# Weight sums of a Strassen feed-forward by accumulating DMAs instead of vector instructions

## The chip, the cores and the metric

The kernel runs on one core of a Trainium2 chip. The metric is the device time of one execution in microseconds; the median of three runs counts. The engines are TensorE (PE, with PEld for its weight loads), VectorE (DVE), ScalarE (ACT), GpSimd (POOL) and SyncE (SP), which issues most DMAs. Each engine works through its own queue in order; semaphores tie the queues together.

## The reference

A decoder trunk of two pre-norm layers on 512 tokens of width 1024, with 16 learned tokens put in front (L = 528). Layer 0 mixes tokens by causal pooling, layer 1 by stick-breaking attention. Each layer ends with a feed-forward part of 2816 hidden features, which is what the change touches. All is float32.

```python
def swiglu(h, w_gate, w_up, w_down):
    return (jax.nn.silu(h @ w_gate) * (h @ w_up)) @ w_down
...
    for i in range(DEPTH):
...
        h = h + mix
        h = h + swiglu(rmsnorm(h, norm_ffn[i]), ffn_w_gate[i], ffn_w_up[i], ffn_w_down[i])
    h = rmsnorm(h, final_norm)
    return h[:, N_META:]
```

## The kernel before

Activations lie feature-major: `hT` is eight chunks of 128 features by 528 tokens. TensorE multiplies float32r values, so each operand is split into two parts: `hi` is a cast on ACT, `lo` the difference on DVE (`wsplit`, lines 88 to 101, for weights). `mm3` (line 118) makes three products per weight block: hi x hi, hi x lo, lo x hi. The hi and lo parts of weights lie in two rings of NW = 8 buffers, each 128 x 512 and so the work of one product of four blocks.

`ffn` (line 289) runs once per layer over 22 hidden tiles of 128 features, in rounds of two or four (`ROUNDS`). A hidden tile is made by `plain` (the first three) or by `strassen`. The latter takes gate and up together as a 2 x 2 block product: rows gate and up, inner halves of the width, columns the two halves of the tokens. Seven products of 12 matmuls stand for eight. They need four sums of weight blocks, s1 = u1 + u2, s2 = s1 - g1, s3 = g1 - u1 and s4 = g2 - s2, where g1, g2, u1, u2 are the halves of the gate and up weights of the tile, 128 x 512 each. The sums are made by GpSimd for tiles below `POOL_SUMS` = 6 and by DVE from there. The seven weights are then split as `ws_0` to `ws_6`; the last figure says which product (1: s2, 2: s1, 4: s3, 5: s4). The products add up in three PSUM tiles `pa`, `pb`, `pc`, and `keep` copies them on ACT (`m`) between products where a part sum is needed later.

On the tokens' side, `operands` (line 362) makes seven operands `xh`, `xl` from the normed chunks `xn` and four differences `t`. GpSimd makes half of the `xn` and all `t`. After each hidden tile some chunks of the down projection of the round before run (`pd`, weights `rd`, split as `wd`).

Raw weights come in by SP: `rgate` and `rup` for two hidden tiles (256 columns, 1 MB) and `rd` for four chunks, all from one ring of three buffers `wraw`.

The code is written in program order, but the order on each engine is set by a scheduler when the program is built, within the limits of the data and the buffers; on the chip it is fixed.

Of the kernel before, what the change touches and what calls it, by code (L numbers as in the profile page):

```python
# [32 lines left out]
POOL_SUMS = 6  # L33
# Chunks of the normed h that GpSimd makes.
POOL_CHUNKS = (4, 5, 6, 7)
# [16 lines left out]
def f32(ap):  # L52
    return ap.bitcast(F32)
# [3 lines left out]
def trunk(ctx: ExitStack, tc: tile.TileContext, x, meta, x_t, gain, pool_w, w_qkv, w_o, w_gate, w_up, w_down,  # L57
          c_ident, c_band, c_mband, c_mask, out_t):
    """gain: the norms' gains and the mixer's scale, feature p of chunk c in row p; x_t: meta and x, feature-major."""
# [21 lines left out]
    def wraw(src, name, eng=None):  # L81
        n, m = src.shape[1], src.shape[2]
        raw = main.tile([P, n * m], F32, tag="wraw", name=name, bufs=3)
        v = raw.rearrange("p (a b) -> p a b", a=n)
        (eng or nc.sync).dma_start(out=v, in_=src)
# [17 lines left out]
    class Cols:  # L103
        """128-column units of a weight [rows, cols], loaded n units at a time."""
# [13 lines left out]
    def mm3(outs, wh, wl, xh, xl, start, stop, more=False):  # L118
        """outs: list of (psum AP, column slice); accumulates w.T @ x exactly to float32's accuracy."""
        for i, (w, xx) in enumerate(((wh, xh), (wh, xl), (wl, xh))):  # L120
            for o, sl in outs:
                nc.tensor.matmul(o, lhsT=w, rhs=xx[:, sl], start=start and i == 0, stop=stop and i == 2,  # L122
                                 skip_group_check=more)
# [31 lines left out]
    class Norm:  # L155
        """Splits h*gain into float32r parts and sums the squares of h over the chunks, chunk by chunk."""
# [21 lines left out]
    def norm_bcast(accs, name, tag):  # L178
        """rstd of every token on all partitions (accs: tiles that add up to the squares of all chunks)."""
# [10 lines left out]
    # ================= layer 0: pooling mixer =================  # L190
    HV = (slice(0, HALF), slice(HALF, L))
    norm = Norm(16, "f0")
    with tc.tile_pool(name="start", bufs=1) as sp, phase("ps0", one=8):
# [7 lines left out]
        pwr = main.tile([P, 2, 4, 256], F32, tag="wraw", name="pwr", bufs=3)  # L201
# [8 lines left out]
        for k in range(2):  # L210
            nc.sync.dma_start(out=pwr[:, k], in_=pool_w[0, :, k * P:(k + 1) * P, :].rearrange("g p d -> p g d"))
# [5 lines left out]
        band = sp.tile([P, 4, BAND], F32R, name="band")  # L217
        nc.vector.tensor_copy(band[:, :, 0:BOFF], zero)
        nc.vector.tensor_copy(band[:, :, BOFF + 144:BOFF + 288], zero)
        nc.vector.tensor_copy(band[:, :, BOFF + 288:], zero[:, :, 0:BAND - BOFF - 288])  # L220
# [53 lines left out]
        pws = [wsplit(pwr[:, k], f"pw{k}", nc.gpsimd) for k in range(2)]  # L274
# [13 lines left out]
    # ================= feed-forward =================  # L288
    def ffn(layer, gcol, norm, after):
        """Gate and up projections of a column tile are one 2 x 2 block product (rows: gate, up; inner: the two halves  # L290
        of D; columns: the two halves of the tokens), done with seven block products instead of eight (Strassen in
        Winograd's form); the first PLAIN tiles go plainly."""
# [9 lines left out]

        def raw_gu(kind, f):
            if f % 2 == 0:
                raws[kind] = wraw(rows[kind][:, f * P:(f + 2) * P].rearrange("(k p) f -> p k f", p=P),
                                  f"r{kind}{layer}_{f}")
            return raws[kind][:, :, (f % 2) * P:(f % 2 + 1) * P]

        def down_w(r, c):
            f0, f1 = ROUNDS[r]  # L310
            if c % 4 == 0:
                raws["down"] = wraw(rows["down"][f0 * P:f1 * P, c * P:(c + 4) * P].rearrange("(k p) f -> p k f", p=P),
                                    f"rd{layer}_{r}_{c}")
            return wsplit(raws["down"][:, :, (c % 4) * P:(c % 4 + 1) * P], f"wd{layer}_{r}_{c}")
# [12 lines left out]
        with tc.tile_pool(name=f"ffn{layer}", bufs=1) as fp:  # L327
# [34 lines left out]
            def operands():  # L362
                """The seven operands on the tokens' side, from the normed h."""
                rb = fst[0]
                for m in range(4):
                    xn = []
                    for c in (m, m + 4):
                        t = fp.tile([P, L], F32, tag="xn", name=f"xn{c}", bufs=2)
                        gc = gains[:, gcol + c:gcol + c + 1]
                        if c in POOL_CHUNKS:  # L370
                            nc.scalar.activation(t[:, tok], hT[c][:, tok], AF.Copy, scale=gc)
                            nc.gpsimd.tensor_tensor(out=t[:, tok], in0=t[:, tok], in1=rb[:, tok], op=ALU.mult)
                        else:
                            nc.vector.scalar_tensor_tensor(t[:, tok], hT[c][:, tok], gc, rb[:, tok], op0=ALU.mult,
                                                           op1=ALU.mult)
# [3 lines left out]
                    for o, a, b in ((t1, b12, b11), (t2, b22, t1), (t3, b22, b12), (t4, b21, t2)):  # L379
                        nc.gpsimd.tensor_tensor(out=o, in0=a, in1=b, op=ALU.subtract)  # L380
# [4 lines left out]
            def strassen(f):  # L385
                g, u = raw_gu("gate", f), raw_gu("up", f)
                a11, a12, a21, a22 = g[:, 0:4], g[:, 4:8], u[:, 0:4], u[:, 4:8]
                sums = [fp.tile([P, 4, P], F32, tag="sums", name=f"s{i}", bufs=4) for i in range(4)]
                s1, s2, s3, s4 = sums
                for o, a, b, op in ((s1, a21, a22, ALU.add), (s2, s1, a11, ALU.subtract), (s3, a11, a21, ALU.subtract),  # L390
                                    (s4, a12, s2, ALU.subtract)):
                    (nc.gpsimd if f < POOL_SUMS else nc.vector).tensor_tensor(out=o, in0=a, in1=b, op=op)
                wa11, ws2, ws1, wa12, ws3, ws4, wa22 = [wsplit(src, f"ws{f}_{i}") for i, src in
                                                        enumerate((a11, s2, s1, a12, s3, s4, a22))]
# [27 lines left out]
                tt(out=m6, in0=m6, in1=m1, op=ALU.add)  # L422
                tt(out=g[:, b], in0=pc, in1=m6, op=ALU.add)
                nc.scalar.activation(sg[:, b], g[:, b], AF.Silu)
                tt(out=u[:, a], in0=pb, in1=m1, op=ALU.add)
                tt(out=m67, in0=m67, in1=m1, op=ALU.add)
                tt(out=u[:, b], in0=m67, in1=m5, op=ALU.add)
# [45 lines left out]
    # ================= layer 1: stick-breaking attention =================  # L473
    with tc.tile_pool(name="att", bufs=1) as ap, phase("ps2", one=2, two=3):
# [13 lines left out]
        def proj(p):  # L488
            """Steps that make q, k (both heads of the pair stacked on partitions) and v, token-major, all split."""
# [61 lines left out]
        def scores(p, hd, q, k):  # L551
            """Weights a (query-major strip) of one head."""
# [21 lines left out]
        def turned(p, hd, sg):  # L574
            """The weights key-major, split."""
# [195 lines left out]
```

## Time and profile before

| | us |
|---|---|
| Runs | 1093.41, 1097.08, 1097.87 (median 1097.08) |
| Span of the profiled execution | 1094.6 |
| PE busy in it | 1047.0 |
| DVE busy | 872.4 |
| ACT busy | 574.4 |
| POOL busy | 286.5 |

The span is the time from the first to the last instruction of one execution that was profiled; the runs are whole executions, so the median stands 2.5 us above that span. The mean granted clock of TensorE is 0.981. Layer 0's feed-forward lies at about 43 to 420 us, the attention at 420 to 715, layer 1's feed-forward behind it. A row of a group reads: line, engine, operation, out<-in, sizes, count, then busy time, mean ns of one, idle time of the engine before them and what ended it. Matmul durations overlap, so a mean of 285 ns of one doesn't say how often one can start.

### The profile page before, as it was taken

Reading aid. Unit: us, or ns where it says so; the run is one execution under the profiler, and the core shown is the slowest. Engines: PE = TensorE matmul, PEld = TensorE weight load, DVE = VectorE, ACT = ScalarE, POOL = GpSimd, SP = SyncE. Lnnn points to the kernel's source line nnn. Section 1 sums busy time; section 2 is a strip of 40 time slices with the busy share of each in tenths; the row PEclk is TensorE's granted clock in tenths of the full one; section 3 lists DMA queues with packets and bytes.
Section 4 is the critical chain, followed back from the end, with each engine's and each line's share of the span. In section 5 each row is a group of like instructions: output and inputs, shape, how many; then the busy total and the mean of one; then the engine's idle time right before and its main releaser. Section 6 shows DMA issues by size and latency. Waiting matters only on the chain.

```text
span 1094.6 us, 18510 instructions
## 1 busy us (share of the span) xinstructions
PE 1047.0 (96%) x7222; PEld 964.1 (88%) x7222; DVE 872.4 (80%) x1420; ACT 574.4 (52%) x1119; POOL 286.5 (26%) x301
## 2 busy tenths in 40 slices
PE   9898899999999999999999999987899999999996
PEld 6897899999999998878888887766899999999995
DVE  7899887888877776776898878799887877787855
ACT  6655454455455454755555565456455445454544
POOL 2646100000000022554566656456400000000002
PEclk8999899999999999999999999999899999999999
DMA  9103332223333222221211112211133333322312
GB/s 328 60 1 97 116 116 85 71 84 110 116 117 116 76 80 77 59 58 48 68 39 58 38 41 97 78 58 38 59 118 114 116 116 116 115 67 90 101 54 77
DMA packets 92343, 95.09 MB, mean 87 GB/s; under 512 B 2240, under 2 KB 79312, under 8 KB 92256
## 3 DMA queue, kind: packets, MB, share of 16 engines
q1 hardware_dynamic: 90992, 92.78, 26.4%
q8 instruction: 56, 0.92, 0.3%
q10 hardware_dynamic: 1264, 1.14, 0.3%
q14 instruction: 31, 0.25, 0.1%
HBM read 91.82 MB, written 2.10 MB: 86 GB/s over the span
## 4 chain that ended last, share of the span: by engine, by line
PE 79%; DVE 13%; issue 4%; POOL 3%; ACT 1%; DMA 1%; SPq 0%; DVEq 0%; POOLq 0%; ACTq 0%
PE pd L122 21%; PE pb L122 14%; PE pj L122 11%; PE pc L122 9%; PE pa L122 9%; PE pp L122 2%; PE po L617 2%; DVE kp L570 2%; PE z L563 2%; PE pw L122 2%; PE z L562 1%; POOL t L380 1%; DVE sg L571 1%; DVE xl L383 1%; PE t L578 1%
## 5 line engine op out<-in xcount | busy, mean ns | idle before, releaser
L325 DVE TENSOR_TENSOR h<-pd,h 128x264 f32<-128x264 f32 (+2 forms) x152 | 74.6, 493 | 31.8 <-PE pd L122 31.5
L706 POOL TENSOR_TENSOR fsq<-fsq,fsq 128x256 f32<-128x256 f32 x8 | 6.2, 779 | 288.7 <-ACT fsq L702 288.6
L477 POOL MEMSET estrip<- 128x1360 bf16 x1 | 1.2, 1232 | 280.5 <-DVE hl L338 280.5
L569 POOL TENSOR_TENSOR sg<-sg,masks 128x128 f32<-128x128 f32 x64 | 49.7, 801 | 63.7 <-ACT sg L566 60.3
L570 DVE TENSOR_TENSOR_SCAN kp<-kp,estrip 128x1360 f32<-128x1360 f32 x16 | 52.1, 3255 | 3.0 <-ACT kp L566 2.9
L97 ACT CAST ws_5h<-s 128x512 fp32r<-128x512 f32 x38 | 23.6, 620 | 47.6 <-PE pb L122 31.1
L122 PE MATMUL pa<-xl,ws_0h 128*128 128x264 f32 (+1 forms) x152 | 43.3, 285 | 3.4 <-DVE xl L383 3.3
L122 PE MATMUL pa<-xh,ws_0h 128*128 128x264 f32 (+1 forms) x152 | 43.1, 284 | 3.6 <-ACT xh L382 3.6
L122 PE MATMUL pb<-xh,ws_1h 128*128 128x264 f32 (+1 forms) x152 | 43.6, 287 | 0.8 <-ACT xh L382 0.8
L122 PE MATMUL pc<-xh,ws_5h 128*128 128x264 f32 (+1 forms) x152 | 44.0, 290 | 0.0
L122 PE MATMUL pc<-xl,ws_2h 128*128 128x264 f32 (+1 forms) x152 | 43.1, 284 | 0.9 <-DVE xl L383 0.9
L122 PE MATMUL pc<-xl,ws_5h 128*128 128x264 f32 (+1 forms) x152 | 44.0, 289 | 0.0
L122 PE MATMUL pb<-xh,ws_4l 128*128 128x264 f32 (+1 forms) x152 | 43.9, 288 | 0.0
L122 PE MATMUL pc<-xh,ws_5l 128*128 128x264 f32 (+1 forms) x152 | 43.8, 288 | 0.0
L122 PE MATMUL pb<-xl,ws_4h 128*128 128x264 f32 (+1 forms) x152 | 43.7, 288 | 0.0
L122 PE MATMUL pb<-xh,ws_4h 128*128 128x264 f32 (+1 forms) x152 | 43.6, 287 | 0.0
L122 PE MATMUL pb<-xl,ws_1h 128*128 128x264 f32 (+1 forms) x152 | 43.5, 286 | 0.0
L122 PE MATMUL pb<-xh,ws_1l 128*128 128x264 f32 (+1 forms) x152 | 43.5, 286 | 0.0
L122 PE MATMUL pa<-xh,ws_3h 128*128 128x264 f32 (+1 forms) x152 | 43.0, 283 | 0.4 <-ACT m L404 0.4
L122 PE MATMUL pc<-xh,ws_2h 128*128 128x264 f32 (+1 forms) x152 | 43.2, 284 | 0.0
L122 PE MATMUL pa<-xh,ws_0l 128*128 128x264 f32 (+1 forms) x152 | 43.2, 284 | 0.0
L122 PE MATMUL pc<-xh,ws_2l 128*128 128x264 f32 (+1 forms) x152 | 43.2, 284 | 0.0
(1219 smaller groups left out, 4453.2 us busy)
## 6 DMA issues: line engine op xcount, KB each, us to landing
rgate<-in_ffn_w_gate_dram SPq DMA_DIRECT2D x22, 1024.0 KB, 5.3
rup<-in_ffn_w_up_dram SPq DMA_DIRECT2D x22, 1024.0 KB, 5.3
rd<-in_ffn_w_down_dram SPq DMA_DIRECT2D x20, 1024.0 KB, 5.5
wqr<-in_sb_w_qkv_dram SPq DMA_DIRECT2D x8, 512.0 KB, 3.8
wkr<-in_sb_w_qkv_dram SPq DMA_DIRECT2D x8, 512.0 KB, 3.7
wvr<-in_sb_w_qkv_dram SPq DMA_DIRECT2D x8, 512.0 KB, 3.9
h<-in_x_t_dram SPq DMA_DIRECT2D x8, 264.0 KB, 6.7
x<-in_x_dram SPq DMA_DIRECT2D x4, 512.0 KB, 5.6
```

Source lines behind the costliest of these rows:

```text
L97: nc.scalar.copy(hi, v[:, j:j + w])
L122: nc.tensor.matmul(o, lhsT=w, rhs=xx[:, sl], start=start and i == 0, stop=stop and i == 2, skip_group_check=more)
L325: nc.vector.tensor_tensor(out=hv, in0=pd, in1=hv, op=ALU.add)
L380: nc.gpsimd.tensor_tensor(out=o, in0=a, in1=b, op=ALU.subtract)
L383: nc.vector.tensor_tensor(out=xl[i][:, m, :], in0=o, in1=f32(xh[i][:, m, :]), op=ALU.subtract)
L562: nc.tensor.matmul(o, lhsT=q[hd][:, qs], rhs=k[hd][:, k0:k1], start=True, stop=False)
L563: nc.tensor.matmul(o, lhsT=q[hd][hs, qs], rhs=k[2][hs, k0:k1], start=False, stop=True)
L569: nc.gpsimd.tensor_tensor(out=sg[:, c:c + P], in0=sg[:, c:c + P], in1=masks[:, 0], op=ALU.mult)
L570: nc.vector.tensor_tensor_scan(kp[:, ::-1], kp[:, ::-1], estrip[:, ::-1], 1.0, op0=ALU.mult, op1=ALU.max)
L571: nc.vector.tensor_tensor(out=sg[:, 0:STRIP - 1], in0=sg[:, 0:STRIP - 1], in1=kp[:, 1:STRIP], op=ALU.mult)
L578: nc.tensor.transpose(o, sg[:, c0:c0 + n], ident)
L617: nc.tensor.matmul(po[:, 0, i0 * P:512], lhsT=lw, rhs=a, start=t == 0 and j == 0, stop=t == 4)
```

## The change

The sums of weights are no longer made by vector instructions. `add` issues, on GpSimd's queue, a DMA that reads 128 x 512 weights from HBM and adds them to what lies in the destination. u1 becomes in turn u1 + u2, then + g1, then + g2; g1 becomes g1 + u1. Each state is split before the next addition overwrites it. The gate rows are thereby taken with the other sign (s2 has + g1, and s3 and s4 change sign), which the combining steps after the products make good by subtracting. The order of the products changes (2 and 3 ahead of 1, and 6 ahead of 5).

Weights are loaded per hidden tile, 128 columns or 512 KB per load, `rd` per two chunks. The ring `wraw` has NRAW = 6 buffers of half the size; `rup` has two buffers of its own in the layer's pool, whose space is used by the pooling or the attention before. GpSimd makes no `xn`, `t` or low parts of weights in the feed-forward and in the pooling any more; DVE does. The zeros of `band` are written by one GpSimd memset. Comments are removed, so lines from 100 to 300 move by two, later ones by up to five.

```diff
+NRAW = 6
...
-    def wraw(src, name, eng=None):
+    def wraw(src, name, eng=None, pool=None):
         n, m = src.shape[1], src.shape[2]
-        raw = main.tile([P, n * m], F32, tag="wraw", name=name, bufs=3)
+        raw = (pool or main).tile([P, n * m], F32, tag="wraw", name=name, bufs=2 if pool else NRAW)
...
-        zero = sp.tile([P, 4, 144], F32, name="zero")
-        nc.gpsimd.memset(zero, 0.0)
+        band = sp.tile([P, 4, BAND], F32R, name="band")
+        nc.gpsimd.memset(f32(band), 0.0)
...
-        pws = [wsplit(pwr[:, k], f"pw{k}", nc.gpsimd) for k in range(2)]
+        pws = [wsplit(pwr[k], f"pw{k}") for k in range(2)]
...
         def raw_gu(kind, f):
-            if f % 2 == 0:
...
+            return wraw(col(kind, f), f"r{kind}{layer}_{f}", pool=fp if kind == "up" else None)
...
-                eng = nc.gpsimd if f < 2 else None
-                parts = [wsplit(raw_gu(kind, f), f"w{kind}{f}", eng) for kind in ("gate", "up")]
+                parts = [wsplit(raw_gu(kind, f), f"w{kind}{f}") for kind in ("gate", "up")]
...
-                    for o, a, b in ((t1, b12, b11), (t2, b22, t1), (t3, b22, b12), (t4, b21, t2)):
-                        nc.gpsimd.tensor_tensor(out=o, in0=a, in1=b, op=ALU.subtract)
+                    for o, a, b, op in ((t1, b11, b12, ALU.subtract), (t2, b22, t1, ALU.add),
+                                        (t3, b12, b22, ALU.subtract), (t4, b21, t2, ALU.subtract)):
+                        nc.vector.tensor_tensor(out=o, in0=a, in1=b, op=op)
...
             def strassen(f):
                 g, u = raw_gu("gate", f), raw_gu("up", f)
-                a11, a12, a21, a22 = g[:, 0:4], g[:, 4:8], u[:, 0:4], u[:, 4:8]
-                sums = [fp.tile([P, 4, P], F32, tag="sums", name=f"s{i}", bufs=4) for i in range(4)]
-                s1, s2, s3, s4 = sums
-                for o, a, b, op in ((s1, a21, a22, ALU.add), (s2, s1, a11, ALU.subtract), (s3, a11, a21, ALU.subtract),
-                                    (s4, a12, s2, ALU.subtract)):
-                    (nc.gpsimd if f < POOL_SUMS else nc.vector).tensor_tensor(out=o, in0=a, in1=b, op=op)
-                wa11, ws2, ws1, wa12, ws3, ws4, wa22 = [wsplit(src, f"ws{f}_{i}") for i, src in
-                                                        enumerate((a11, s2, s1, a12, s3, s4, a22))]
+                g1, g2, u1, u2 = g[:, 0:4], g[:, 4:8], u[:, 0:4], u[:, 4:8]
+                src = {(kind, i): col(kind, f)[:, 4 * i:4 * i + 4] for kind in ("gate", "up") for i in range(2)}
+
+                def add(o, kind, i):
+                    nc.gpsimd.dma_start(out=o, in_=src[kind, i], accum_op=ALU.add)
...
+                wa22 = split(6, u2)
+                add(u1, "up", 1)
+                wa11 = split(0, g1)
+                add(g1, "up", 0)
+                ws1 = split(2, u1)
+                add(u1, "gate", 0)
+                wa12 = split(3, g2)
+                ws2 = split(1, u1)
+                add(u1, "gate", 1)
+                ws3 = split(4, g1)
+                ws4 = split(5, u1)
...
                 prod(pa, wa11, 0, True)
                 m1 = keep(pa, "m1")
-                prod(pb, ws2, 1, True)
-                m6 = keep(pb, "m6")
                 prod(pc, ws1, 2, True)
                 m5 = keep(pc, "m5")
                 prod(pa, wa12, 3, False)
+                prod(pb, ws2, 1, True)
+                m6 = keep(pb, "m6")
                 prod(pb, ws3, 4, False)
                 m67 = keep(pb, "m67")
+                prod(pb, wa22, 6, False)
                 prod(pc, ws4, 5, False)
-                prod(pb, wa22, 6, False)
```

The scheduler's new order is seen at three places in the middle of layer 0. On GpSimd's queue the changed kernel has, around tile 14 (the figure behind `rup` and `rgate` is the hidden tile; an out<-in of `rup<-..up` is the first sum, of `rup<-..gate` the second and third, of `rgate<-..up` the gate's):

```order
L384 DMA rgate_13_3168<-in_ffn_w_up_dram 128x4x128
L384 DMA rup_14_3382<-in_ffn_w_up_dram 128x4x128
L384 DMA rup_13_3170<-in_ffn_w_gate_dram 128x4x128 x2
L384 DMA rgate_14_3380<-in_ffn_w_up_dram 128x4x128
L384 DMA rup_15_3594<-in_ffn_w_up_dram 128x4x128
L384 DMA rup_14_3382<-in_ffn_w_gate_dram 128x4x128 x2
```

Before, GpSimd had nothing here; now the first sum of the next tile stands ahead of the second and third sums of the tile before it. In layer 1 the gate's sum and the next tile's first sum change places, so that both stand between.

SP's queue, same place, in the changed kernel, loads each tile's gate, the up weights of one tile earlier, and `rd`:

```order
L83 DMA rgate_15_3592<-in_ffn_w_gate_dram 128x8x128
L83 DMA rup_14_3382<-in_ffn_w_up_dram 128x8x128
L83 DMA rd_3_2_3738<-in_ffn_w_down_dram 128x4x256
L83 DMA rgate_16_3804<-in_ffn_w_gate_dram 128x8x128
L83 DMA rup_15_3594<-in_ffn_w_up_dram 128x8x128
```

The load of `rup` 15 waits for the buffer of `rup` 13: for its third sum's DMA and for both halves of the split `ws_5` of tile 13. Before, one load per two tiles stood here.

On ACT, the changed kernel from the split of tile 13's second weight sum (`ws_2`, that is s1) on; `m` are the copies of part sums of tile 12 and 13, `hh` is the hidden tile's own split:

```order
L95 CAST ws_2h_3182<-rup_13_3170 128x512
L426 ACTIVATE sg_3088<-pa_2992 128x264
L95 CAST ws_3h_3187<-rgate_13_3168 128x512
L409 COPY m_3061<-pb_2993 128x264
L432 ACTIVATE sg_3088<-g_3087 128x264
L95 CAST ws_1h_3191<-rup_13_3170 128x512
L95 CAST ws_4h_3196<-rgate_13_3168 128x512
L331 CAST hh_3098<-u_3089 128x528
L409 COPY m_3219<-pa_3204 128x264
L409 COPY m_3233<-pc_3206 128x264
L95 CAST ws_5h_3200<-rup_13_3170 128x512
```

Before, the casts of `ws_1`, `ws_2`, `ws_4` and `ws_5` read sums `s` made by DVE in one go; now the casts of `ws_2`, `ws_1` and `ws_5` read the same buffer `rup`, with one DMA between each two.

More of the change, by code (lines that the diff above doesn't have):

```diff
@@ L31 @@
 PLAIN = 3
-POOL_SUMS = 6
-POOL_CHUNKS = (4, 5, 6, 7)
+NRAW = 6
 NW = 8
@@ L197, in trunk @@
         band_raw = sp.tile([P, 4, 144], F32, name="bandr")
-        zero = sp.tile([P, 4, 144], F32, name="zero")
-        nc.gpsimd.memset(zero, 0.0)
+        band = sp.tile([P, 4, BAND], F32R, name="band")
+        nc.gpsimd.memset(f32(band), 0.0)
         mband = sp.tile([META, 4, 32], F32, name="mband")
-        pwr = main.tile([P, 2, 4, 256], F32, tag="wraw", name="pwr", bufs=3)
+        pwr = [main.tile([P, 4, 256], F32, tag="wraw", name=f"pwr{k}", bufs=NRAW) for k in range(2)]
         nc.sync.dma_start(out=xt[0], in_=x[0, 0:P, :])
@@ L210, in trunk @@
         for k in range(2):
-            nc.sync.dma_start(out=pwr[:, k], in_=pool_w[0, :, k * P:(k + 1) * P, :].rearrange("g p d -> p g d"))
+            nc.sync.dma_start(out=pwr[k], in_=pool_w[0, :, k * P:(k + 1) * P, :].rearrange("g p d -> p g d"))
         for c in range(KC):
@@ L301, in ffn, with col @@
         raws = {}
+        def col(kind, f):
+            return rows[kind][:, f * P:(f + 1) * P].rearrange("(k p) f -> p k f", p=P)
         def raw_gu(kind, f):
-            if f % 2 == 0:
-                raws[kind] = wraw(rows[kind][:, f * P:(f + 2) * P].rearrange("(k p) f -> p k f", p=P),
-                                  f"r{kind}{layer}_{f}")
-            return raws[kind][:, :, (f % 2) * P:(f % 2 + 1) * P]
+            return wraw(col(kind, f), f"r{kind}{layer}_{f}", pool=fp if kind == "up" else None)
         def down_w(r, c):
             f0, f1 = ROUNDS[r]
-            if c % 4 == 0:
-                raws["down"] = wraw(rows["down"][f0 * P:f1 * P, c * P:(c + 4) * P].rearrange("(k p) f -> p k f", p=P),
+            if c % 2 == 0:
+                raws["down"] = wraw(rows["down"][f0 * P:f1 * P, c * P:(c + 2) * P].rearrange("(k p) f -> p k f", p=P),
                                     f"rd{layer}_{r}_{c}")
-            return wsplit(raws["down"][:, :, (c % 4) * P:(c % 4 + 1) * P], f"wd{layer}_{r}_{c}")
+            return wsplit(raws["down"][:, :, (c % 2) * P:(c % 2 + 1) * P], f"wd{layer}_{r}_{c}")
         def down(r, c, hid, w=None, sls=pieces, tag="d"):
@@ L369, in operands @@
                         gc = gains[:, gcol + c:gcol + c + 1]
[L370 to L375, printed above, removed]
+                        nc.vector.scalar_tensor_tensor(t[:, tok], hT[c][:, tok], gc, rb[:, tok], op0=ALU.mult,
+                                                       op1=ALU.mult)
                         xn.append(t)
@@ L421, in strassen @@
                 nc.scalar.activation(sg[:, a], pa, AF.Silu)
[L422 removed]
+                tt(out=m6, in0=m1, in1=m6, op=ALU.subtract)
+                tt(out=m67, in0=m67, in1=m1, op=ALU.subtract)
+                tt(out=u[:, b], in0=m67, in1=m5, op=ALU.subtract)
+                tt(out=u[:, a], in0=pb, in1=m1, op=ALU.subtract)
                 tt(out=g[:, b], in0=pc, in1=m6, op=ALU.add)
                 nc.scalar.activation(sg[:, b], g[:, b], AF.Silu)
[L425 to L427 removed]
                 tt(out=u, in0=sg, in1=u, op=ALU.mult)
```

6 lines of the change are left out of this document (2 added, 4 removed).

## The prediction

> **What bounds the kernel now.** I read the page's head first (busy time, the slices), then the chain that ended last, the waits and the DMA issues, and then cut the span into stages.
>
> ```profile
> PE 1047.0 (96%) x7222; PEld 964.1 (88%) x7222; DVE 872.4 (80%) x1420; ACT 574.4 (52%) x1119; POOL 286.5 (26%) x301
> PE 79%; DVE 13%; issue 4%; POOL 3%; ACT 1%; DMA 1%; SPq 0%; DVEq 0%; POOLq 0%; ACTq 0%
> ```
>
> TensorE is nearly always busy, and 79% of the chain is its work. In the stretch of each feed-forward layer in which one hidden tile follows the other evenly, it never stops:
>
> ```profile
> 163.20:388.58 225.38, 225.38 (x1854) 225.38 (x1853) 176.28 (x335) 111.35 (x225) 0.00 (x0) 1.00 0.30 97
> 881.50:1036.49 154.99, 154.99 (x1082) 144.47 (x1081) 122.56 (x221) 77.71 (x161) 0.00 (x0) 1.00 0.31 103
> ```
>
> The columns are length, then busy time (instructions) of PE, PEld, DVE, ACT and POOL, the granted clock, DMA share and GB/s. Both stretches run from one `pd` piece of the chain to another, at the same place of a tile: 14 tiles in 225.38 us make **16.1 us per tile** in layer 0, 10 tiles in 154.99 us make **15.5 us** in layer 1. PE is busy for all of both at clock 1.00; DVE has 78% and 79%, POOL nothing, DMA 0.30. So in 38 tiles, some 600 us, only PE's own work counts: less work on DVE gains nothing there. The number of matmuls and their columns don't change.
>
> Where PE does wait is at the start of each feed-forward layer, while the operands are made:
>
> ```profile
> 40.00:120.00 80.00, 66.50 (x506) 64.28 (x505) 77.23 (x116) 44.67 (x96) 47.64 (x36) 0.97 0.17 54
> 112.00:116.00 4.00, 0.73 (x3) 0.73 (x4) 4.00 (x5) 0.00 (x0) 2.25 (x2) 0.80 0.00 0
> 116.00:120.00 4.00, 4.00 (x20) 4.00 (x19) 3.92 (x8) 2.34 (x5) 0.00 (x0) 0.50 0.01 4
> 720.00:800.00 80.00, 70.43 (x376) 61.23 (x375) 72.35 (x106) 41.27 (x91) 40.86 (x32) 0.92 0.18 55
> ```
>
> There DVE is full (77.23 and 72.35 of 80 us), POOL works beside it, and PE idles 13.5 and 9.6 us. After the hole at 112 its clock is 0.50 for four microseconds. That is all the gain that can be had: about 15 us per layer.
>
> **The change part by part.** First, what DVE loses in the even stretch: four sums per tile from tile 6 on.
>
> ```profile
> L392 DVE TENSOR_TENSOR s<-s,rgate 128x512 f32<-128x512 f32 x15 | 10.3, 684 | 0.2
> L98 DVE TENSOR_TENSOR ws_5l<-s,ws_5h 128x512 fp32r<-128x512 f32 x15 | 10.2, 681 | 0.0
> L338 DVE TENSOR_TENSOR hl<-u,hh 128x528 fp32r<-128x528 f32 x17 | 11.9, 698 | 0.0
> L97 ACT CAST ws_5h<-s 128x512 fp32r<-128x512 f32 x15 | 9.3, 621 | 27.2 <-PE pb L122 27.2
> L422 DVE TENSOR_TENSOR m<-m,m 128x264 f32<-128x264 f32 x16 | 6.8, 425 | 0.0
> ```
>
> 4 x 0.68 = 2.7 us of DVE per tile go, worth 0 since PE hides them. The sign changes and the other order of the products cost 0: as many instructions of the same forms.
>
> Second, the layer's start. POOL's work goes to DVE: 16 differences of 128x264 at 0.43 us, four `xn` of 128x528 at 0.70 (as `hl`) and eight low parts at 0.68, together 15 us per layer. But POOL no longer stands beside DVE:
>
> ```profile
> L383 DVE TENSOR_TENSOR xl<-xn,xh 128x264 fp32r<-128x264 f32 x12 | 8.2, 710 | 0.0
> L383 DVE TENSOR_TENSOR xl<-t,xh 128x264 fp32r<-128x264 f32 x16 | 7.9, 524 | 0.0
> L98 DVE TENSOR_TENSOR ws_5l<-s,ws_5h 128x512 fp32r<-128x512 f32 x2 | 2.5, 1264 | 0.0
> ```
>
> These rows are from 55 to 115 us. The same forms take 0.425 and 0.681 us where POOL is silent, so 28 `xl` carry 4 us too much, and a split up to 0.6 us; some 14 splits and the `xn` make it about 13 us. Gained and lost on DVE are alike. I take **0** for both starts; the ends are -15 us each (all of PE's loss gone) and +15 us (nothing of the slowing goes away). The three zero copies of `band` on DVE become one memset on POOL, and four low parts of `pw` go to DVE: about 1 us either way.
>
> ```profile
> 15.61 0.38 SPq L85 DMA_DIRECT2D rup<-in_ffn_w_up_dram  x1
> 41.02 0.28 PE L122 MATMUL mix<-ph,pw1l 128*128 128x264 f32 x1
> 55.07 0.51 PE L122 MATMUL pp<-f0ul,wgate0h 128*128 128x264 f32 x2 [1.67 <-DVE f0ul L166]
> 101.49 1.29 POOL L392 TENSOR_TENSOR s<-rup 128x512 f32<-128x512 f32 x1 [6.68 <-DMA rup<-in_ffn_w_up_dram]
> ```
>
> `rup` of tile 0 was issued at 15.61 us. It now waits until the pooling's buffers are free, which is after the last `mix` product, at 41.3. Loaded by about 46 and split by 49, it stands before the norm's last chunk lets PE go on at 55.07: cost 0. Without that cover it would be the load and two splits, 7 us.
>
> Third, the sums by DMA. In the even stretch each tile now has a chain through one buffer of `rup`, and the orders shown above fix it. On POOL `rup` of tile 15 (first sum) stands ahead of the second and third sums of tile 14. It must wait for the load of `rup` 15, which needs the buffer of tile 13, so the split of tile 13's last sum. Behind it the second sum of 14 is queued, then the split `ws_1`, the third sum, the split `ws_5` of 14, the load of `rup` 16, and so on. One turn per tile:
>
> split + load L + issue q + sum A + split + sum A.
>
> If it is longer than 16.1 us, it sets the time: PE's product `pc<-ws_5` waits for it each tile, and two buffers can't run ahead. Behind the waiting cast of `ws_5` on ACT stand the casts of `wd` for the down projection, of the next tile's `ws_6` and `ws_0`, and the copy `m` that lets PE write `pb` again. A split is one ACT cast and one DVE difference, 0.62 + 0.68 = 1.3 us. For the rest I have only the loads of the other kind:
>
> ```profile
> wqr<-in_sb_w_qkv_dram SPq DMA_DIRECT2D x6, 512.0 KB, 3.8
> wo2r<-in_sb_w_o_dram SPq DMA_DIRECT2D x4, 256.0 KB, 2.8
> pwr<-in_pool_w_dram SPq DMA_DIRECT2D x2, 512.0 KB, 7.5
> rgate<-in_ffn_w_gate_dram SPq DMA_DIRECT2D x4, 1024.0 KB, 6.2
> rgate<-in_ffn_w_gate_dram SPq DMA_DIRECT2D x7, 1024.0 KB, 5.4
> 6.38 6.78 SPq L213 DMA_DIRECT2D h<-in_x_t_dram  x8
> ```
>
> The last column of the first five is the time from issue to landing (`pwr` and the first `rgate` row from 0 to 140 us, where loads queue; the second `rgate` from 140 to 400). L is a `wqr` load, as large and in the same 512-byte pieces: 3.8, plus 0.5 for more traffic (the two `rgate` rows differ by 0.8): **4.3 us**. q: eight issues of SP in a row took 6.78 us, **0.85** each, and POOL makes its own in software. A, of 256 KB, appears nowhere. From below it is the plain 256 KB load, 2.8 us. From above I take the slowest load of the profile, 7.5. It reads 256 KB from HBM and 256 KB of the tile, in 512-byte pieces: by bytes and pieces it is nearest to the `wqr` row, 3.8, plus the issue 0.85 and the same 0.5: **5.1 us**.
>
> Turn: 2 x 1.3 + 4.3 + 0.85 + 2 x 5.1 = **18.0 us**, 1.9 over 16.1. In layer 1 POOL's order also has the gate's sum between, another 0.85: 18.8, 3.3 over 15.5. From tile 5, the first whose `rup` waits for a used-up one, 17 tiles follow in each layer: 17 x 1.9 + 17 x 3.3 = 32 + 56 = **+88 us**.
>
> Loads per 128 columns halve the pieces, which costs nothing by bytes: these queue rows are of 420 to 680 us (512-byte pieces mostly) and 140 to 400 us (1 and 2 KB).
>
> ```profile
> q1 hardware_dynamic: 23260, 13.89, 18.0%
> q1 hardware_dynamic: 22218, 25.59, 30.5%
> ```
>
> 13.89 MB take 18.0% and 25.59 MB 30.5%: 77 and 84 MB per full share. The sums bring 1 MB per tile to the 1.5 MB that are loaded: at the plain price 0.30 becomes 0.50, at three times for the sums 0.90.
>
> The Trainium skill's page "DMA: Bandwidth & Descriptors", section "Anatomy of one DMA — SWDGE (gpsimd) path", gives a DMA issued by GpSimd about 2.0 us plus its bytes over 436 GB/s, an estimate of 2.6 us here. No run here shows such a DMA yet, nor does the page price an accumulation. By it the turn would be 13.0 us and hidden, which is the first rival's result; the 2.8 us of the plain row says so too.
>
> **The rivals.** *The sums are hidden.* With A up to (16.1 - 7.75) / 2 = 4.2 us in layer 0 (3.45 in layer 1, with both issues) the turn stays under PE's tile. Then only the starts count: 1097 - 30 to 1097 + 30, most likely about 1088, since `rup` of tile 4, for which POOL's sums waited 6.68 us ahead of the hole at 112, is loaded earlier. For it: the 2.8 us row. Against it: a sum waits, is issued, reads two sources and must land before the split, twice in a row. *Each sum costs far more*, 7.5 us, when a DMA engine can't overlap reading the tile with writing it: turns of 22.8 and 23.6 us, 17 x (6.7 + 8.1) = +251, 1348 us. *The change doesn't shorten DVE's part*: that DVE's relief helps the even stretch speaks against PE's 225.38 of 225.38.
>
> **How the numbers follow.** The profiled execution has a span of 1094.6 us; the median of the runs is 1097.08, so 2.5 us lie around it, and I add to the median: 1097 + 88 = **1185 us**. Chances: the chain decides with A between 4 and 6.5 us, 0.57 (1116 to 1280: at 4 it is 17 x 1.1 = 19 us in layer 1 alone, at 6.5 it is 17 x (4.7 + 6.1) = +183); sums dearer than that, 0.20; sums hidden, 0.23, of which 0.14 come out over 0.5% faster, 0.07 within 0.5% (what a measurement of this kernel can tell from no change) and 0.02 slower. So faster 0.14, same 0.07, slower 0.79. The range reaches from the hidden case to a good part of the dear one, 1086 to 1300.
>
> **What would show it.** Right: in the even stretch a tile takes about 18 us, PE is busy for 82 to 89% of it (15.5 of 18.8, 16.1 of 18.0), its idle time stands before `pc<-ws_5` or `pb<-ws_1`, ended by ACT or DVE splits whose own wait ends at a sum's DMA; POOL's queue shows sums landing after about 5 us. Wrong: PE full at 16.1 us per tile (A under 4), or sums above 7 us. The starts are right if PE's idle there is within 5 us of before, and DVE's `xl` falls to 0.43 us.

## The result

The changed kernel takes **1271.17 us** (median of 4 runs, 1265.29 to 1275.19), the kernel before, run beside it, 1095.82 us: the ratio is 1.159, with a 95% interval of 1.157 to 1.162. The forecast was 1185 us with a range of 1086 to 1300, so the direction and the range were right; of the +175 us it had named +88.

The page of the changed kernel, in its parts on queues and on the chain that ended last, and then five groups that wait long (count, then busy us, mean ns of one, idle us ahead, and who ended it):

```profile
q0 software_dynamic: 80256, 39.86, 25.6%
q1 hardware_dynamic: 148400, 92.79, 24.9%
DMA 40%; PE 31%; DVE 10%; issue 9%; POOL 5%; ACT 3%; POOLq 0%; ACTq 0%; SPq 0%; DVEq 0%
L384 POOL DMA_DIRECT2D rup<-in_ffn_w_gate_dram x76 | 124.1, 1633 | 223.5 <-DVE ws_1l L96 213.1
L95 ACT CAST ws_1h<-rup 128x512 fp32r<-128x512 f32 x38 | 23.6, 620 | 183.5 <-DMA rup<-in_ffn_w_gate_dram 183.5
L95 ACT CAST ws_5h<-rup 128x512 fp32r<-128x512 f32 x38 | 23.5, 618 | 160.4 <-DMA rup<-in_ffn_w_gate_dram 160.4
L120 PE MATMUL pc<-xh,ws_5h 128*128 128x264 f32 (+1 forms) x152 | 52.0, 342 | 34.0 <-ACT ws_5h L95 34.0
L120 PE MATMUL pb<-xh,ws_1h 128*128 128x264 f32 (+1 forms) x152 | 45.5, 299 | 15.4 <-ACT ws_1h L95 15.0
```

DMA, 1% of that chain before, is its largest part. ScalarE's casts of `ws_1` and `ws_5` wait 344 us in all, each for a sum from the gate rows; TensorE's idle time stands at `pc<-ws_5` and `pb<-ws_1`. How long a tile takes is read from the casts of `ws_5`: the first and the last in one stretch of layer 0, from ScalarE's timeline (start, duration):

```profile
L95 ACT CAST ws_5h<-rup x15: 617/617/621, 157.7 to 447.4; 128x512 fp32r<-128x512 f32 x15
```

Fifteen casts are fourteen turns: (447.4 - 157.7) / 14 = **20.7 us** per tile, where it was 16.1. The same reading gives 21.6 us in layer 1 (fourteen turns from 903.72 to 1205.55). One such turn in the chain that ended last (start, duration, what):

```profile
238.71 0.63 ACT ws_5h L95
...
239.36 0.70 DVE ws_5l L96
...
240.08 4.05 DMA rup<-in_ffn_w_up_dram
...
244.66 0.74 POOL rup L384
245.41 6.80 DMA rup<-in_ffn_w_gate_dram
...
252.24 1.69 issue
...
253.94 5.81 DMA rup<-in_ffn_w_gate_dram
...
259.77 0.63 ACT ws_5h L95
```

Split of `ws_5`, load of the next `rup`, issue of that tile's first sum on GpSimd, then the second sum of this tile, which had stood behind it in the queue, its split (the 1.69 us of "issue": ScalarE's timeline has the cast of `ws_1` at 252.30), the third sum, and `ws_5` again: 21.06 us. TensorE is nowhere in it.

### The profile page after: what moved, and what is told of

Same layout as the page of the kernel before. It is cut to its first block, busy times and chain, and to the rows that moved or that the text cites. A ratio compares the mean times of both kernels' runs of the same rounds, so it can differ in the third digit from the quotient of the medians.

```text
span 1273.3 us, 18922 instructions
## 1 busy us (share of the span) xinstructions
PE 1117.5 (88%) x7222; PEld 1014.3 (80%) x7222; DVE 776.4 (61%) x1349; ACT 553.0 (43%) x1111; POOL 370.4 (29%) x369
## 3 DMA queue, kind: packets, MB, share of 16 engines
q0 software_dynamic: 80256, 39.86, 25.6%
## 4 chain that ended last, share of the span: by engine, by line
DMA 40%; PE 31%; DVE 10%; issue 9%; POOL 5%; ACT 3%; POOLq 0%; ACTq 0%; SPq 0%; DVEq 0%
DMA rup<-in_ffn_w_gate_dram 33%; PE pj L120 10%; DMA rup<-in_ffn_w_up_dram 7%; PE pd L120 5%; PE pp L120 5%; POOL rgate L384 2%; PE po L622 2%; POOL rup L384 2%; PE pw L120 2%; PE z L568 1%; ACT ws_5h L95 1%; DVE kp L575 1%; PE z L567 1%; DVE ws_5l L96 1%; PE pa L120 1%
## 5 line engine op out<-in xcount | busy, mean ns | idle before, releaser
L384 POOL DMA_DIRECT2D rup<-in_ffn_w_gate_dram x76 | 124.1, 1633 | 223.5 <-DVE ws_1l L96 213.1
L384 POOL DMA_DIRECT2D rup<-in_ffn_w_up_dram x38 | 48.9, 1287 | 319.4 <-DMA rup<-in_ffn_w_up_dram 103.4
L96 DVE TENSOR_TENSOR ws_1l<-rup,ws_1h 128x512 fp32r<-128x512 f32 x38 | 26.3, 692 | 139.7 <-ACT ws_1h L95 138.8
L96 DVE TENSOR_TENSOR ws_5l<-rup,ws_5h 128x512 fp32r<-128x512 f32 x38 | 26.3, 692 | 137.7 <-ACT ws_5h L95 137.6
L384 POOL DMA_DIRECT2D rgate<-in_ffn_w_up_dram x38 | 58.9, 1550 | 162.5 <-DVE ws_0l L96 162.5
L120 PEld LDWEIGHTS pc<-xh,ws_5h 128*128 128x128 f32 x152 | 36.4, 239 | 37.3 <-ACT ws_5h L95 36.9
L120 PE MATMUL pa<-xl,ws_3h 128*128 128x264 f32 (+1 forms) x152 | 49.3, 324 | 0.0
L120 PE MATMUL pb<-xh,ws_6h 128*128 128x264 f32 (+1 forms) x152 | 44.5, 293 | 5.3 <-ACT m L409 5.3
L120 PE MATMUL pa<-xh,ws_3l 128*128 128x264 f32 (+1 forms) x152 | 49.0, 322 | 0.0
L96 DVE TENSOR_TENSOR ws_3l<-rgate,ws_3h 128x512 fp32r<-128x512 f32 x38 | 26.1, 688 | 33.9 <-ACT ws_3h L95 33.7
```

Of the source, the lines that this page charges most:

```text
L96: (eng or nc.vector).tensor_tensor(out=lo, in0=v[:, j:j + w], in1=f32(hi), op=ALU.subtract)
L384: nc.gpsimd.dma_start(out=o, in_=src[kind, i], accum_op=ALU.add)
```

## The experiments

Two questions: whether this loop of waits sets the time (chain theory), or rather the summing DMAs' bytes and issues (traffic theory), the new order of the products, or the finer loads. And what decides the length of the loop. Each kernel is the changed one, or one made from it, with the main lines of the edit shown; the expectations were written before it ran. A time with an interval rests on four or ten runs, any other on one; the four runs of the changed kernel lie 10 us apart.

### The sums on VectorE

```diff
-                add(u1, "up", 1)
+                tadd(u2, u1)        # nc.vector.tensor_tensor, in place; the splits read u2
...
-                add(g1, "up", 0)
-                add(u1, "gate", 0)
+                tadd(u2, g1)
+                tadd(g1, u1)
-                add(u1, "gate", 1)
+                tadd(u2, g2)
```

> The four weight sums of a feed-forward tile are made in place by VectorE from buffers that are there anyway; the negated gate rows, the loads per 128 columns and all else of the change stay. Chain theory (the loop through the one rup buffer: load, issues on GpSimd, two sums one after the other, splits): the loop is gone, since no split waits for a transfer that starts only after the split before; a tile is bound by TensorE again at 15.5 to 16.5 us and the time is 1080 to 1110 us. Traffic theory (the summing DMAs' bytes and issues as such): the same, 1080 to 1110. Order theory (the products stand in another order, pb twice in a row with m copied between): most of the loss stays, 1200 us or more. Loads theory (loads per 128 columns and small side changes): 1200 or more.

Measured: **1080.42 us**, 0.985 of the kernel before (interval 0.982 to 0.989), the fastest of this study. TensorE is full again in the even stretch:

```profile
157.75:380.00 222.25, 222.25 (x1828) 222.25 (x1827) 179.73 (x330) 110.28 (x222) 0.00 (x0) 1.00 0.32 98
```

(Columns: stretch and length; busy time of PE, PEld, DVE, ACT and POOL; granted clock, DMA share, GB/s.) The loads per 128 columns and the new product order are all in this kernel, so neither costs the 175 us. Chain and traffic are still alike.

### The same sums, but nobody waits for them

```diff
 e_dve, and behind the last split of a tile:
+                add(g1, "up", 1)
+                add(g2, "up", 0)
+                add(g1, "gate", 0)
+                add(g2, "gate", 1)
```

> As e_dve (sums on VectorE), and besides four summing DMAs of 256 KB per tile go into the two gate buffers once these have been read for the last time: the same issues on GpSimd and the same bytes as in the change, but nothing in the tile reads what they make. Chain theory: within 2% of e_dve, 1080 to 1125 us (the gate buffers come free some us later, which the loads ahead hide). Traffic theory: the time of the change, 1230 to 1290.

Measured: 1081.02 us. Its page has the same packets and bytes on the software queue as the changed kernel:

```profile
q0 software_dynamic: 80256, 39.86, 30.1%
PE 1043.7 (97%) x7222; PEld 958.8 (89%) x7222; DVE 879.1 (81%) x1501; ACT 569.6 (53%) x1111; POOL 370.8 (34%) x369
```

80256 packets and 39.86 MB, as in the changed kernel, and the time is 0.6 us over e_dve's median, within the spread of its runs (1079.33 to 1081.24). The traffic theory falls: these DMAs cost time only where something waits for them.

### One sum fewer in the loop, then two

```diff
 e_two:
-                add(u1, "gate", 1)
+                tadd(u1, g2)
 e_one, besides:
-                add(u1, "gate", 0)
+                tadd(u1, g1)
```

> The change with the last sum of the chain (the one for ws_5) made by VectorE; the other three stay summing DMAs, so one serial transfer and one split fewer stand in the loop. Chain theory: the loop is 20.7 - (6.8 + 0.7) + 0.6 = about 14 us in layer 0 and 15 in layer 1, below TensorE's 16.1 and 15.5, so nearly all of the loss goes: 1085 to 1130 us. Traffic theory: a quarter of the loss goes, about 1225.

> The change with the second and third sum of the chain made by VectorE; the first sum and the gate's stay summing DMAs (two per tile). Chain theory: no sum of tile f is queued behind one that waits for the load of tile f+1; a load, an issue and a first sum (4.5 + 0.5 + 0.75 + 5.8) have a tile and more to pass in, so TensorE bounds the tile again: 1078 to 1095 us. If every sum that a split waits for costs its share: (1176 + 1080) / 2 = 1130 or more.

Measured: e_two 1176.27 us, e_one 1094.50. e_one fits, e_two does not: without its third sum the tile still took (419.4 - 165.5) / 14 = 18.1 us, where 14 were expected. The chain of e_two (start, duration, what), and below it the landing times of its three sums:

```profile
241.94 4.54 DMA rup<-in_ffn_w_up_dram
...
247.08 0.50 POOL rup L384
...
247.80 0.75 POOL rgate L384
248.55 6.62 DMA rup<-in_ffn_w_gate_dram
...
255.19 0.63 ACT ws_1h L95
...
255.84 0.69 DVE ws_1l L96
...
256.80 0.68 DVE rup L390
257.48 0.60 DVE ws_4l L96
258.08 0.35 DVE u L433
...
258.46 0.71 DVE u L436
259.17 0.60 DVE ws_5l L96
```

```profile
rup<-in_ffn_w_up_dram POOLq DMA_DIRECT2D x38, 256.0 KB, 4.5
rgate<-in_ffn_w_up_dram POOLq DMA_DIRECT2D x38, 256.0 KB, 5.7
rup<-in_ffn_w_gate_dram POOLq DMA_DIRECT2D x38, 256.0 KB, 6.6
```

It is the same loop, load, first sum's issue, second sum, without the third. But the expectation took off 6.8 us, the second sum's length, where the third's 5.81 fell away. It put 0.6 us in its place, and VectorE's queue puts 1.7 us more between the addition (`rup`, ended at 257.48) and `ws_5l`, from `ws_4l` to `u`. And all three sums are now issued in one burst, 0.75 us apart, so the one that the loop waits for is the last: 6.6 us. By the medians of the second list, sums issued at 0, 0.75 and 1.5 land at 4.5, 6.45 and 8.1 us, some 1.8 us apart, as if one went behind the other.

In e_one the loss against the kernel before is gone, but not for the reason in its expectation. The gate's sum of a tile does stand behind the next tile's first sum, which waits for its load (255.70 and 258.66 on GpSimd's timeline). But then it still waits 1.68 us for VectorE's own sum, which reads the same `g1` first, so the load costs it nothing. The two sums are issued some 3 us apart and land after 4.5 and 4.6 us (medians).

### What the addition in the transfer costs

```diff
-                    nc.gpsimd.dma_start(out=o, in_=src[kind, i], accum_op=ALU.add)
+                    nc.gpsimd.dma_start(out=o, in_=src[kind, i])
```

> The change with the same four DMAs from the same queue as plain copies: the addition is left out, so those products use other weights. It measures what the addition in the transfer costs. Chain theory: each turn has two of them, so the time falls by 2 x 34 x (summing minus plain, from issue to landing); at 4.0 us instead of 6.0 that is 2 x 34 x 2.0 = 136 us, to about 1135, and if both take as long the time stays at 1271. Traffic theory: the bytes read are the same; unless the addition itself is slow in the queue the time stays at 1240 to 1275.

Measured: 1120.47 us, 151 us under the changed kernel, a little more than the 136 expected. Its queue row and issues:

```profile
q0 software_dynamic: 12160, 39.86, 11.7%
rup<-in_ffn_w_gate_dram POOLq DMA_DIRECT2D x76, 256.0 KB, 3.9
rup<-in_ffn_w_up_dram POOLq DMA_DIRECT2D x38, 256.0 KB, 3.8
rgate<-in_ffn_w_up_dram POOLq DMA_DIRECT2D x38, 256.0 KB, 4.1
```

A plain copy lands after 3.8 to 4.1 us wherever it stands, a sum after 4.6 to 5.8 in the changed kernel (medians). The time of the packets goes with it: 11.7% of 1118.7 us over 152 copies is 0.86 us of all 16 engines each, 25.6% of 1273.3 over 152 sums is 2.1 us.

### The products in the order of before

```diff
 (the order of the changed kernel: pa ws_0, pc ws_2, pa ws_3, pb ws_1, pb ws_4, pb ws_6, pc ws_5)
+                prod(pb, ws2, 1, True)         # behind the first pa
+                prod(pb, wa22, 6, False)       # last
```

> The change with its products in the order of before (pb of s2 right behind the first, the last two exchanged), the sums by DMA kept. Chain theory: the splits' order and the loop stay, so the time stays at 1255 to 1285 us; TensorE only waits in another place. Order theory (pb twice in a row with the copy m between costs PE time): 1240 or less.

Measured: 1278.62 us, with (447.4 - 151.7) / 14 = 21.1 us per tile. TensorE's order is no part of the loss, and this kernel keeps the loop.

### GpSimd's queue in another order

```diff
+                with tc.issue_after(last.pop()):     # the third sum of the tile before
                     add(u1, "up", 1)
```

> The change with one edge of order on GpSimd's queue: the first sum of tile f+1 is issued behind the third sum of tile f, not ahead of the second. All sums, bytes and the buffers stay. Chain theory: the load of rup leaves the loop, which becomes third issue, first sum, split, second sum, split, third issue: 2 x 5.8 + 2 x 1.3 + 0.75 + about 1 for the waits = 16 us (17 to 18 if the gate's sum rides along in one of them), beside TensorE's 16.1 and 15.5, so most of the loss goes: 1085 to 1165 us, likeliest 1110. If only the number of summing DMAs and their latency counts, not what they are queued behind: 1250 to 1285.

Measured: 1224.45 us, some 47 less, where 106 to 186 were expected. The load has left the loop, and the tile takes (438.5 - 151.1) / 15 = 19.2 us all the same. ScalarE's timeline between two casts of `ws_5` tells what took its place (start, duration, idle ahead):

```profile
264.50 0.62 ACT L95 CAST ws_5h<-rup 128x512 fp32r<-128x512 f32 x1 [3.61 <-DMA rup<-in_ffn_w_gate_dram]
265.03 0.61 ACT L95 CAST wd_4h<-rd 128x512 fp32r<-128x512 f32 x1
...
266.34 0.62 ACT L95 CAST ws_6h<-rup 128x512 fp32r<-128x512 f32 x1
...
267.13 0.63 ACT L95 CAST ws_0h<-rgate 128x512 fp32r<-128x512 f32 x1
...
268.60 0.62 ACT L95 CAST ws_2h<-rup 128x512 fp32r<-128x512 f32 x1 [0.56 <-PE pa L120]
...
275.79 0.62 ACT L95 CAST ws_1h<-rup 128x512 fp32r<-128x512 f32 x1 [3.78 <-DMA rup<-in_ffn_w_gate_dram]
...
283.77 0.62 ACT L95 CAST ws_5h<-rup 128x512 fp32r<-128x512 f32 x1 [3.95 <-DMA rup<-in_ffn_w_gate_dram]
```

The cast of `ws_5` waits at the head of ScalarE's queue for the third sum. Behind it stands all that the next tile needs ahead of its second sum, `ws_6`, `ws_0`, `ws_2`; so the second sum starts only after this tile's third: 4.1 us of ScalarE, 1.6 to the second sum's issue (270.24 on GpSimd's timeline), 5.6 for it, 1.6 to the third's (277.43), 6.3 for that. Taking the load out of GpSimd's queue left a longer loop through ScalarE's queue, with both sums in it. The loop that was expected is there too, and as long as expected: the first sum, issued at 259.39, had landed 6.5 us later, 2.7 us ahead of the cast of `ws_2`, so that the way from one issue of a third sum (258.64) to the next (277.43) has 18.8 - 2.7 = 16.1 us of its own.

A first reading of these rows was another: `ws_2` waited 0.56 and, a turn later, 1.85 us for TensorE to free a pair of split-weight buffers.

```diff
 e_swap with
-NRAW = 6
+NRAW = 5
-NW = 8
+NW = 9
```

> e_swap with nine pairs of split-weight buffers instead of eight (and five raw buffers instead of six to make room). In e_swap the cast of ws_2 waited for TensorE to free a pair, so the loop was ws_5, TensorE's next products, ws_2, second sum, ws_1, third sum, ws_5, 19.0 us. Chain theory: with one pair more ws_2 waits for one product less, 1.5 to 2.5 us a turn on 34 turns: 1224 - (51 to 85) = 1140 to 1175 us. If the two sums and splits alone make up the 19 us, whatever frees the pair: 1215 to 1235.

Measured: 1232.79 us, no gain, so the pairs of buffers do not set the turn. `ws_2` no longer waited for TensorE there, but GpSimd issued the second sum 0.75 us behind the gate's instead of 1.35, and it took 7.0 us (274.99 to 282.03) instead of 5.6. What the sixth raw buffer would have been worth beside nine pairs was not tried.

### ScalarE's queue in another order

```diff
                 ws1 = split(2, u1)
+                if pend:
+                    pend.pop()()        # ws_5, its product and what follows, of the tile before
...
-                ws4 = split(5, u1)
-                prod(pc, ws4, 5, False)
...
+                pend.append(finish)
```

> The change with the last step of a tile (split of ws_5, its product and what follows) written behind the split ws_2 of the next tile, so that ScalarE's queue has ws_2, m, ws_5 and GpSimd's has second sum of f, first of f+1, third of f. All four sums stay summing DMAs with the same bytes. Chain theory (the loops through GpSimd's and ScalarE's queues): a turn is now split, load, first sum of f+2 issued, third sum of f+1 = 1.3 + 5 + 1.5 + 6 = 13.8 us, or split, load, first sum, ws_2, ws_5 = 1.3 + 5 + 5.8 + 1.1 = 13.2, both under TensorE's 15.5 and 16.1: 1078 to 1110 us. If two serial sums per tile cost their 20 us whatever is queued around them: 1200 or more.

> e_swap and e_late together: the first sum of tile f+1 behind the third of f on GpSimd, and ws_5 behind the next ws_2 on ScalarE. Chain theory: the load is out of the loop, but all three sums are in it: third issue, first sum, ws_2, second sum, ws_1, third issue = 0.75 + 6 + 1.7 + 0.75 + 6.3 + 1.7 = 17.2 us, 1.1 and 1.7 over TensorE's: 1080 + 48 = about 1128 (1100 to 1150), slower than e_late although its load no longer waits. If only ScalarE's queue mattered: as e_late. If the sums' number matters: 1200 or more.

Measured: e_late **1101.82 us**, 1.005 of the kernel before (1.002 to 1.007): 169 of the 175 us are back, with the same four summing DMAs per tile. In its even stretch (columns as above):

```profile
163.20:388.00 224.80, 224.72 (x1846) 224.51 (x1845) 146.09 (x279) 110.85 (x225) 69.16 (x54) 1.00 0.85 159
```

TensorE is full, with DMA busy for 0.85 of the stretch. With both loops no longer than TensorE's tile, the four sums are hidden there. The time is still 21 us over e_dve's; where they are lost is told below, with the layer's start.

e_swaplate took 1189.27 us, not 1128. That it is slower than e_late was expected and the reason too: the next tile's first sum, its second, and the issue of its third one after the other, turn by turn. The length of the sums was not expected:

```profile
257.18 8.23 DMA rup<-in_ffn_w_up_dram
...
265.50 0.63 ACT ws_2h L95
...
266.15 0.70 DVE ws_2l L96
...
267.14 8.00 DMA rup<-in_ffn_w_gate_dram
```

The first sums take 8.0 to 8.8 us in the five turns from 218 to 305 us and the second ones 6.4 to 8.0, where 6 and 6.3 were expected. A first sum stands 0.75 us behind a third one, and two loads of 512 KB are issued right after it (257.64 and 259.52 on SyncE's timeline). Both seem to count: in e_swap, where the same sum stands as close behind a third one but with one load beside it, its median is 6.9 us, here 7.9. They were not tried one by one.

### Where the 15 us come from by which e_dve beats the kernel before

```diff
 e_pool: e_dve with the operands' 16 differences and four scaled chunks per layer on nc.gpsimd
 e_starts: e_pool, and
+                eng = nc.gpsimd if f < 2 else None                  # splits of plain tiles
+                    (nc.gpsimd if f < 6 else nc.vector).tensor_tensor(...)    # tiles 3 to 5
```

> e_dve (sums on VectorE) with GpSimd given back its part of the operands at each layer's start: 16 differences and four scaled chunks per layer, as before the change. It asks where the 15 us come from by which e_dve beats the kernel before. If they come from the starts (GpSimd's arithmetic beside VectorE slows both, and TensorE waits for operands): 1088 to 1098 us. If they come from the loads per 128 columns, the earlier loads or the order of the products: 1078 to 1084.

> e_pool with the rest of GpSimd's arithmetic given back too: the splits of the first two tiles' gate and up weights, and the four sums of tiles 3 to 5, in both layers. Loads, product order and buffers stay as in the change. If the 14 us by which e_pool beats the kernel before come from this arithmetic (GpSimd's sums take 1.5 us against 0.68, slow VectorE beside them, and the splits behind them are late): 1092 to 1100 us. If they come from the loads per 128 columns, their earlier start or the products' order: 1078 to 1085.

Measured: e_pool 1082.00 us (0.987 of before, 0.984 to 0.990), the second alternative; e_starts 1091.66 (0.995, 0.993 to 0.997), at the edge of the first. The operands on GpSimd cost 1.6 us, within the spread; the first tiles' splits and sums cost 9.7. These two were moved together and are not told apart. The 6 us that e_starts is still ahead of the kernel before were not followed further: finer and earlier loads, the products' order, the low parts of `pw` on VectorE and one memset are what is left.

## Why the prediction came out as it did

**The bound and VectorE's relief: right.** e_late has 30 us less of VectorE in the even stretch than the kernel before (146 and 176 in stretches alike) and does no more matmuls there (1846 and 1854): the relief is worth 0. The loads per 128 columns cost nothing either: e_dve has them all.

**The layer's start: 0 was right for a kernel with summing DMAs, for a reason that it did not have.** Its signs came true: in the window from 40 to 120 us TensorE idles 9.5 us, where it idled 13.5, `xl` fell to 0.42 us, and `rup` of tile 0 delayed nothing. e_dve, without the sums by DMA, gains 15 us for both layers together. The step counted GpSimd's operands against VectorE's slowing, and e_pool agrees that these cancel. What it left out is what GpSimd's splits and sums of the first tiles cost, 9.7 us by e_starts; at about 1.5 us each they may simply be late, which was not tried by itself. But the kernels whose sums come by DMA don't keep that gain. The same window of layer 0 in the kernel before, e_dve, e_one and e_late (columns as above; the number in the first brackets counts TensorE's products):

```profile
40.00:160.00 120.00, 106.50 (x830) 104.28 (x829) 110.04 (x181) 65.56 (x139) 47.64 (x36) 0.97 0.26 83
40.00:160.00 120.00, 112.72 (x888) 110.95 (x889) 111.96 (x229) 66.57 (x142) 0.00 (x0) 0.97 0.33 97
40.00:160.00 120.00, 109.05 (x827) 104.80 (x827) 98.38 (x206) 61.98 (x136) 14.29 (x11) 0.97 0.51 117
40.00:160.00 120.00, 108.39 (x818) 103.79 (x818) 93.95 (x197) 63.13 (x136) 27.21 (x21) 0.97 0.66 132
```

By 120 us e_one and e_late, with 560 and 540 products, are ahead of the kernel before with its 506; by 160 us they have lost it again, some 60 to 70 products behind e_dve. With 8.2 products per us in the even stretch that is 7 to 9 us in layer 0. Since TensorE is full in the even stretches of both, the rest of the 14 and 21 us that they take more than e_dve should lie at layer 1's start. Which wait of the first tiles it is was not followed.

**The loop: right in every link; its sums were mis-sized.** The order of GpSimd's queue, the load through the used-up buffer, two sums one after the other: the turn shown has these links and no other. (In layer 1 at least one turn of the chain passes through VectorE's queue, from 1011.20 to 1016.79 us, beside the load issued at 1011.92.) Set beside the turn of 21.06 us:

| link | forecast | measured in the turn |
|---|---|---|
| two sums A | 2 x 5.1 | 6.80 + 5.81 |
| load L | 4.3 | 4.05 |
| issue q | 0.85 | 0.53 + 0.74 |
| splits, with their waits | 2 x 1.3 | 1.37 + 1.74 |
| turn | 18.0 | 21.06 |

Of the 3.1 us that are missing, 2.4 are A. The error in A is large in the result because only what stands over TensorE's 16.1 and 15.5 us counts: 18.0 and 18.8 were 1.9 and 3.3 over, 20.7 and 21.6 are 4.6 and 6.1. With these, the same formula gives 17 x 4.6 + 17 x 6.1 = 182 us; against e_dve, the changed kernel without the sums by DMA, they cost 191. So the forecast's +88 stands for +191 and -15 in the result.

A was built from one load's duration plus an issue, as if a sum were alone. The runs show that it isn't a constant: 4.5 us with no other sum ahead (e_one), 6.6 as the third of a burst (e_two), 7.0 right behind another (e_swapnw), 8.2 right behind another and beside two loads (e_swaplate). In the turn shown, the second sum follows the first one's issue by 0.75 us, and 6.80 fits that; the third has no sum ahead, but a load of 512 KB issued 0.34 us after it (254.28 on SyncE's timeline), which would account for 5.81. No experiment tries that by itself, but the changed kernel's own trace agrees: its three third sums with no load issued in their first 2 us (at 81.87, 836.74 and 1219.51) landed after 4.3 to 4.6 us, and those with a load 0.3 to 1 us behind them after 5.5 to 7.2.

**The rule that was weighed: it falls short.** By the Trainium skill's page "DMA: Bandwidth & Descriptors", section "Anatomy of one DMA — SWDGE (gpsimd) path", 256 KB were estimated at 2.6 us and the sums hidden. No DMA issued by GpSimd came near: 3.8 us is the shortest median of a plain copy (e_plain), and 4.5 of a sum (e_one).

**The rivals.** Hidden sums needed A under 4.2 and 3.45 us. The plain copies of e_plain, at 3.9, stand between, with a tile of (397.5 - 163.5) / 14 = 16.7 us, and cost about 40 us against e_dve; so the rival's threshold was near the truth and its A was not. The dear rival put A at 7.5, because the engines would read and write the tile in turn. Its time came a little closer (1348 forecast), by an A that is too large. Its reason is not shown; what is shown is that a sum's packets hold the engines 2.5 times as long as a copy's, while a sum with none ahead lands only 0.7 us later than a copy (4.5 and 3.8 us). The shares of DMA forecast for layer 0, 0.50 to 0.90, hold: 0.68 in the stretch of the loop, 0.85 in e_late.

**What the forecast had seen and not used.** It said that the next tile's `ws_6` and `ws_0` stand behind the waiting cast of `ws_5` on ScalarE. That is a second loop, some 19 us long in e_swap, a little shorter than the first. While the first was there, the first decided; once it was out of the way, this one kept e_swap from its gain.

## What to carry to other kernels

When work moves into a DMA that a split waits for, draw the whole loop through each in-order queue that touches it, the issuing engine's and the waiting engine's, and compare its length with the bound; the DMAs' bytes did nothing here, even at a share of 0.85. Price such a DMA by its place in its queue, not alone. And where a loop is cut in one queue, look for the next one at once: here moving one split in the program brought both down to the bound and gave back 169 of 175 us, while the plain vector addition was faster still.

## What the hardware showed besides

The packets of a summing DMA of 256 KB took 2.1 us of all 16 engines, those of a plain one from the same queue 0.86, and it made 528 packets (80256 over 152) where the plain one made 80.

TensorE's granted clock was 0.91 in the stretch of the loop and 1.00 in the kernel before. Windows of 2 us of the changed kernel, in which `pc<-ws_5` waited 1.50 us from 237.88 to 239.38 (columns as above):

```profile
238.00:240.00 2.00, 0.61 (x3) 0.40 (x3) 0.64 (x2) 1.29 (x3) 0.00 (x0) 1.00 0.10 12
240.00:242.00 2.00, 2.00 (x13) 2.00 (x14) 2.00 (x5) 2.00 (x5) 0.00 (x0) 0.72 0.29 79
242.00:244.00 2.00, 2.00 (x11) 2.00 (x11) 2.00 (x4) 1.00 (x3) 1.24 (x1) 0.50 0.97 275
244.00:246.00 2.00, 2.00 (x17) 2.00 (x17) 1.25 (x5) 0.20 (x1) 1.38 (x3) 0.92 1.06 244
246.00:248.00 2.00, 2.00 (x19) 2.00 (x18) 0.75 (x3) 0.23 (x1) 1.25 (x1) 1.00 1.03 124
```

Ahead of the wait TensorE had been full at 1.00. Behind it the clock is 0.50 for a while, with 11 matmuls in 2 us instead of 19. So the busy share hides the stall: the page says PE 88%, in layer 0's stretch 251 of 290 us, though the work is 14 tiles of 16.1 us, 225. The share of 82 to 89% that the forecast named was met with tiles of 20.7 us, not of 18. It costs nothing in the turn shown, since TensorE is not in that loop. The Trainium skill's page "TensorE: Matmul & The Clock Gate", section "What's actually happening", gives half clock after an idle window of some 3.4 us. This trace agrees on the half clock, but here a wait of 1.50 us was enough.
